# Loading the adaLN modulation weights in half-size column blocks, earlier, and one part of them later

## The chip, the cores and the metric

The kernel runs on one core of a Trainium2 chip. The metric is the device time of one execution in microseconds. TensorE is called PE here, its weight loads PEld, VectorE DVE, ScalarE ACT, GpSimd POOL and SyncE SP. Each engine takes its instructions in order from a queue of its own. SP issues nearly all DMAs.

## The reference: what is computed

Two layers over 256 latent and 256 context tokens of width 1024, in float32. Each layer has six modulation vectors (shift, scale and gate for the mixer, and again for the experts) per condition:

```python
cond_l = silu(c); cond_c = silu(c_ctx)
shift1, scale1, gate1, shift2, scale2, gate2 = split(cond_l @ mod_w[layer] + mod_b[layer], 6)
h = layer_norm(x) * (1 + scale1) + shift1
x = post_norm(ALPHA * x + gate1 * token_mixer(h), ...)
h = layer_norm(x) * (1 + scale2) + shift2
x = post_norm(ALPHA * x + gate2 * moe(h), ...)
```

`mod_w` is 2 x 1024 x 6144. The token mixer projects `h` with `w_in`, runs four branches (windowed attention, a bidirectional Mamba-2 scan, global attention, S5), gates and sums them (`merge`), and multiplies by `w_out`. The experts are 32, with two per token, chosen by a router.

## The kernel before

The work is written out layer by layer in `mixer` and `moe`. A scheduler of the kernel framework turns that text into one fixed order per engine when the kernel is built. It goes by data dependences, by buffers that come free, and by a priority, which is the place in the text; `tc.high_priority(offset=n)` moves what stands inside it n instructions ahead. The attention (scores, softmax, transposes, products) stands in such a block of 3000, because it is traced behind the projections but has a long chain.

The modulation of one layer is cut into three parts i = 0, 1, 2 of 2048 columns of `mod_w`, two vectors each. Part 0 gives shift1 and scale1, which the layer needs first; part 1 gives gate1 and shift2; part 2 gives scale2 and gate2. `mod_part(l, i, ...)` (through `mod_steps`) does a part in eight steps, one for 128 rows of the weight: a DMA of 128 x 2048 floats (1 MB, 8 KB per row) into the tile `modr` (L162), then four matmuls of 512 columns into four groups of 32 rows of the PSUM tile `pm` (L164). The two conditions stand in `cond`, padded to 32 columns. Behind the eighth step DVE adds the bias `mb`, four DMAs store the rows in the DRAM tensor `mods`, and for part 0 `mod_scalars` transposes them into `modT`, from which the layer's first normalisation takes its scalars.

Part (0, 0) is done at the start. The loop behind the attention traces parts (0, 1), (0, 2) and (1, 0) in layer 0, and (1, 1) and (1, 2) in layer 1. The pool `modr` has one buffer, so a load needs the matmuls of the load before it to be over. The PSUM pool `psM` of `pm` has one buffer too; the router's `pcv` and `pcs` use it behind the parts.

Then comes `merge`, a loop over the branches in the order 1, 3, 0, 2: `yr` loads a branch's rows (two buffers), `yh` and `yl` split them for a three-product float32 matmul (L507 to L509), `raw`, `hi` and `lo` do the same to `w_branch`, `gatel` loads the gates, and DVE adds the gated result to `msum`. Behind the second branch stands the router's preparation: `cv` loads shift2 and scale2 from `mods`, `pcv` transposes them, and `wc` and `csum` are built in buffers of `yr`. Behind the merge `pmod.close()` gives the space of `modr` free, `rawo`, `woh` and `wol` prepare `w_out`, and `pout` is the output projection.

Of the kernel before, what the change touches and what calls it, by code (L numbers as in the profile page):

```python
# [11 lines left out]
F32 = mybir.dt.float32  # L12
# [10 lines left out]
KT = 8  # L23
# [15 lines left out]
def part_bcast(ap, n):  # L39

    return bass.AP(tensor=ap.tensor, offset=ap.offset, ap=[[0, n]] + [list(d) for d in ap.ap])
# [11 lines left out]
def trunk(ctx: ExitStack, tc: tile.TileContext, A, out):  # L53
    nc = tc.nc
    V, S, G, T = nc.vector, nc.scalar, nc.gpsimd, nc.tensor
    dma = nc.sync.dma_start
# [8 lines left out]
    def pa(name="pa"):  # L65
        return psA.tile([128, 512], F32, tag="a", name=name)
# [7 lines left out]
    def pm_(name="pm"):  # L74
        return psM.tile([128, 512], F32, tag="m", name=name)

    def tt(o, a, b, op):
        V.tensor_tensor(o, a, b, op=op)  # L78
# [59 lines left out]
    cond = const.tile([128, KT, 32], F32, name="cond")  # L138
# [11 lines left out]
    def mod_part(l, i, wtile, width, mbt):  # L150

        return [ld for ld in mod_steps(l, i, wtile, width, mbt)][-1]

    def mod_steps(l, i, wtile, width, mbt):

        pm = pm_("pm")
        n = width // 512
        for kt in range(KT):
            for j0 in range(0, 4, n):
                w = wtile()  # L160
                c0 = i * 2048 + j0 * 512
                ld = dma(w, A["mod_w"][l, kt * 128:(kt + 1) * 128, c0:c0 + width])  # L162
                for j in range(n):
                    T.matmul(pm[32 * (j0 + j):32 * (j0 + j) + 32, :], cond[:, kt, :], w[:, j * 512:(j + 1) * 512],  # L164
                             start=(kt == 0), stop=(kt == KT - 1))
                yield ld
        mb = mbt()
        V.memset(mb, 0.0)
        for j in range(4):
            src = A["mod_b"][l, (4 * i + j) * 512:(4 * i + j + 1) * 512]  # L170
            dma(mb[32 * j:32 * j + 2], part_bcast(src, 2))
        row = mb
        tt(row, pm, mb, OP.add)
        for j in range(4):
            dma(mods[l, 4 * i + j], row[32 * j:32 * j + 2])
        if i == 0:
            mod_scalars(l, row)
# [3 lines left out]
    def mod_scalars(l, row):  # L181

        pt = pm_("pmt").rearrange("p (a b) -> p a b", a=4)
        for q in range(4):
            T.transpose(pt[:, q], row[:, q * 128:(q + 1) * 128], ident)
        V.tensor_copy(modT[l], pt.rearrange("p q (j r) -> p q j r", j=4)[:, :, :, 0:2])
        ts(modT[l][:, :, 2:4], modT[l][:, :, 2:4], 1.0, None, OP.add)
# [238 lines left out]
    def mixer(l, keep, prev):  # L426
# [6 lines left out]
        gates = pg_.enter_context(tc.tile_pool(name=f"gates{l}", bufs=1, reuse_waits="tile"))  # L433
# [6 lines left out]
        with ExitStack() as pl_:  # L440
# [33 lines left out]
            if prev:  # L474
                prev[1].close()
                modr = pmod.enter_context(tc.tile_pool(name=f"modr{l}", bufs=1, side="right", reuse_waits="tile"))
# [26 lines left out]
        def load_w(c0, n):  # L503
            return [split_w(A["w_in"][l, half * 512:(half + 1) * 512, c0:c0 + n], n) for half in range(2)]
# [86 lines left out]
        w = load_w(C_SB, 256)  # L591
        for i, p in enumerate(proj_fm(w, 0)):
            conv(4 + i, p, 0)
        w = load_w(C_SC, 272)
# [8 lines left out]
        for kt in range(KT):  # L603
            for i, b in enumerate((hhi, hlo)):
                T.matmul(pdf[:32], wdt[:, kt].rearrange("p i c -> p (i c)"), b[:, kt], start=(kt == 0 and i == 0),
                         stop=(kt == KT - 1 and i == 1))
# [35 lines left out]
        for ck in range(2):  # L642
            w = load_w(C_SZ + 256 * ck, 256)
# [7 lines left out]
        with tc.tile_pool(name=f"us{l}", bufs=2, reuse_waits="tile") as wk:  # L651
            for ck in range(2):
                w = load_w(C_SU + 256 * ck, 256)
# [233 lines left out]
        for br, c_q, c_k in ((0, C_AQ, C_AK), (1, C_GQ, C_GK)):  # L887
            for ck in (2, 0, 1):
                w = load_w(c_q + 256 * ck if ck < 2 else c_k, 256)
                for t in range(0 if ck == 2 else t0 // 128, 4):  # L890
                    p = pa("ptm")
# [39 lines left out]
        for n in order:  # L931
            if n == order[3]:
                s5_glu()
            for ck in range(4):
                w = load_w(C_GATE + 1024 * n + 256 * ck, 256)
# [10 lines left out]
        else:  # L946
            tla = ptl.enter_context(tc.tile_pool(name=f"ta{l}", bufs=1, side="right", reuse_waits="tile"))
            modr = pmod.enter_context(tc.tile_pool(name=f"modr{l}", bufs=1, side="right", reuse_waits="tile"))
# [157 lines left out]
                        att_tile(ab[1], pp, wk, late.pop(0))  # L1106
            att_apply(*pend)

        for ml, mi in ((0, 1), (0, 2), (1, 0)) if l == 0 else ((1, 1), (1, 2)):
            mod_part(ml, mi, lambda: modr.tile([128, 2048], F32, tag="modr", name="modr"), 2048,  # L1110
                     lambda: gates.tile([128, 512], F32, tag="gate", name="mb", bufs=4) if l == 0 else modr.tile([128, 512], F32, tag="mb", name="mb"))

        g1 = {qt0 // 2: mod_bc(tla, l, 2, qt0 // 2, "g1")}

# [1 line left out]
        for n in order:  # L1116
# [13 lines left out]
            for ck in range(4):  # L1130
# [5 lines left out]
                for i in range(2):  # L1136
                    g = gates.tile([128, 512 - t0], F32, tag="gate", name="gatel", bufs=4)
                    dma(g, g_d[l, n, 2 * ck + i, :, t0:])
                    p = pa("pm")
# [10 lines left out]
            if n == order[1]:  # L1150
# [26 lines left out]
                T.matmul(pcs, ones, flat, start=True, stop=True)  # L1177
                V.tensor_copy(flat, pcs)


        nt = 4 - qt0
        pmod.close()
# [2 lines left out]
        with ExitStack() as pt_:  # L1185
# [44 lines left out]
            for t in range(nt):  # L1230
                tk = slice(128 * t, 128 * t + 128)
                c = (t + qt0) // 2
# [5 lines left out]
                h = bc.tile([128, D], F32, tag="h2", name="h2")  # L1238
                rt["x1"].append(x)
                for nh in range(2):  # L1240
                    cs = slice(512 * nh, 512 * nh + 512)
                    p = pa("pout")
# [7 lines left out]
                for half in range(2):  # L1250
                    pt = pb("ph2").rearrange("p (a b) -> p a b", a=4)
                    for a in range(4):
                        kt = 4 * half + a
# [690 lines left out]
    for l in range(L):  # L1944
        keep = ExitStack()
        rt = mixer(l, keep, prev)
        prev = moe(rt, keep), keep
# [78 lines left out]
```

## Time and profile before

| | |
|---|---|
| median of 3 runs | 2580.48 us (2578.58 to 2581.49) |
| the profiled execution | 2574.12 us |
| its span, first to last instruction | 2572.2 us |
| PE busy | 2199.5 us, 86% |
| DVE busy | 1403.1 us, 55% |
| ACT busy | 692.3 us, 27% |
| mean granted clock of PE | 0.936 |
| DMA | 710.66 MB, mean 276 GB/s |

Busy times of an engine are the time that its instructions covered; those of PE have modelled ends, since matmuls are pipelined. A wait is the idle time of an engine ahead of an instruction, with what ended it. The granted clock is PE's, as a share of its upper level of 2.4 GHz; 0.5 is the lower one, 1.2 GHz. Times in the rows below are from the span's start. The layers' mixers run from 0 to about 960 us and from about 1540 to 2080 us, each with its experts behind it.

### The profile page before, as it was taken

The numbers are of one execution on the slowest core, as the hardware profiler recorded it, in microseconds if no ns is written. First come the engines' busy times: TensorE is split into PE (matmuls) and PEld (weight loads), VectorE is DVE, ScalarE is ACT, GpSimd is POOL, SyncE is SP. The second block draws the span as 40 slices with busy tenths as digits, with TensorE's granted clock in tenths as the row PEclk, the third lists the DMA queues.
The fourth block names the chain that finished last, engine by engine and source line by source line (L and its number), as shares of the span: only waits on it lengthen the run. The fifth ranks groups of instructions, "written<-read, shape, count | busy, mean of one in ns | idle before, by whom it ended". The sixth has DMA issues, their size and how long they took to land. (4 is left out here: it accounts for less than half of the span.)

```text
span 2572.2 us, 40839 instructions
## 1 busy us (share of the span) xinstructions
PE 2199.5 (86%) x15878; PEld 1514.0 (59%) x15878; DVE 1403.1 (55%) x2787; ACT 692.3 (27%) x1344; POOL 724.5 (28%) x686
## 2 busy tenths in 40 slices
PE   5898997799994988987888747997889879999996
PEld 3687875576651765544444427886777755555553
DVE  7947889956761782000000058466679665454544
ACT  2334422144551301111111113352456311111110
POOL 8989787753210031111111020201133110000000
PEclk8999998899996988999999978998999879999998
DMA  6643477675764768999999965459875689999996
GB/s 247 179 145 120 131 212 199 172 243 169 224 191 159 245 242 347 372 412 407 416 405 415 411 258 171 148 183 262 272 244 149 217 322 384 422 422 421 422 421 271
DMA packets 290516, 710.66 MB, mean 276 GB/s; under 512 B 40014, under 2 KB 199166, under 8 KB 232464
## 3 DMA queue, kind: packets, MB, share of 16 engines
q1 hardware_dynamic: 283600, 694.72, 74.8%
q0 software_dynamic: 5280, 8.05, 1.1%
q10 hardware_dynamic: 1440, 5.24, 0.5%
q8 instruction: 127, 2.08, 0.3%
q14 instruction: 69, 0.57, 0.1%
HBM read 645.82 MB, written 71.37 MB: 279 GB/s over the span
## 5 line engine op out<-in xcount | busy, mean ns | idle before, releaser
L1706 PE MATMUL pgu<-mraw,xgt 128*64 128x256 f32 x4224 | 494.4, 385 | 30.1 <-DMA mraw<-in_moe_w_up_dram 27.0
L1706 PEld LDWEIGHTS pgu<-mraw,xgt 128*64 128x64 f32 x4224 | 298.7, 138 | 220.2 <-DMA mraw<-in_moe_w_up_dram 57.5
L84 DVE SCALAR_TENSOR_TENSOR th<-th,pgu 128x256 f32<-128x256 f32 x132 | 55.5, 421 | 500.5 <-ACT th L1671 498.2
L507 PE MATMUL pfm<-hhi,hi 128*128 128x256 f32 (+1 forms) x832 | 282.9, 344 | 6.0 <-ACT hi L93 4.6
L1726 PE MATMUL pd<-mraw,at 128*64 128x512 f32 x1056 | 251.7, 604 | 39.9 <-DMA mraw<-in_moe_w_down_dram 38.0
L509 PE MATMUL pfm<-hhi,lo 128*128 128x256 f32 (+1 forms) x832 | 280.8, 342 | 4.9 <-DVE lo L78 4.8
L508 PE MATMUL pfm<-hlo,hi 128*128 128x256 f32 (+1 forms) x832 | 283.1, 342 | 2.1 <-DVE hlo L78 2.0
L78 DVE TENSOR_TENSOR lo<-raw,hi 128x1024 fp32r<-128x1024 f32 (+1 forms) x147 | 207.1, 1412 | 74.9 <-ACT hi L93 74.0
L128 POOL TENSOR_TENSOR bnrs<-bnrs,mhalf 128x1 f32<-128x1 f32 x26 | 29.1, 1125 | 688.3 <-DVE bnrs L88 688.3
L93 ACT ACTIVATE hi<-raw 128x1024 fp32r<-128x1024 f32 (+1 forms) x160 | 169.4, 1059 | 195.4 <-PE pfm L508 99.5
L1726 PEld LDWEIGHTS pd<-mraw,at 128*64 128x64 f32 x1056 | 72.2, 136 | 182.1 <-issue 112.7
L507 PEld LDWEIGHTS pfm<-hhi,hi 128*128 128x128 f32 x832 | 158.7, 193 | 33.9 <-ACT hi L93 5.2
L509 PEld LDWEIGHTS pfm<-hhi,lo 128*128 128x128 f32 x832 | 157.6, 191 | 27.2 <-DVE lo L78 6.3
L508 PEld LDWEIGHTS pfm<-hlo,hi 128*128 128x128 f32 x832 | 158.5, 191 | 20.4 <-DVE hlo L78 2.9
L78 DVE TENSOR_TENSOR acc<-acc,po 128x512 f32<-128x512 f32 x124 | 79.6, 683 | 99.7 <-PE po L1814 99.6
L1766 POOL DMA_INDIRECT yb_d<-ye,idx x30 | 29.9, 998 | 294.0 <-ACT ye L93 266.7
L507 PE MATMUL pm<-yh,hi 128*128 128x512 f32 (+1 forms) x256 | 88.5, 360 | 11.6 <-DVE gatel L84 6.4
L508 PE MATMUL pm<-yl,hi 128*128 128x512 f32 (+1 forms) x256 | 91.0, 357 | 5.0 <-DVE yl L78 4.9
L164 PE MATMUL pm<-modr,cond 128*32 128x512 f32 x320 | 61.2, 684 | 38.4 <-DMA modr<-in_mod_w_dram 38.3
L507 PE MATMUL ptm<-hi,hhi 128*128 128x256 f32 x320 | 92.5, 289 | 0.0
L509 PE MATMUL ptm<-hi,hlo 128*128 128x256 f32 x320 | 91.7, 287 | 0.0
L508 PE MATMUL ptm<-lo,hhi 128*128 128x256 f32 x320 | 91.7, 287 | 0.0
(506 smaller groups left out, 4354.9 us busy)
## 6 DMA issues: line engine op xcount, KB each, us to landing
mraw<-in_moe_w_gate_dram SPq DMA_DIRECT2D x132, 1024.0 KB
mraw<-in_moe_w_up_dram SPq DMA_DIRECT2D x132, 1024.0 KB
mraw<-in_moe_w_down_dram SPq DMA_DIRECT2D x132, 1024.0 KB
raw<-in_w_in_dram SPq DMA_DIRECT2D x116, 512.0 KB
modr<-in_mod_w_dram SPq DMA_DIRECT2D x40, 1024.0 KB
modw<-in_mod_w_dram SPq DMA_DIRECT2D x8, 1024.0 KB
gt_d<-gt SPq DMA_DIRECT2D x16, 512.0 KB
q_d<-Q SPq DMA_DIRECT2D x32, 256.0 KB
```

The source lines that it names most:

```text
L78: V.tensor_tensor(o, a, b, op=op)
L84: V.scalar_tensor_tensor(o, a, s, b, op0=op0, op1=op1)
L93: S.activation(o, a, AF.Copy, scale=scale)
L128: G.tensor_tensor(o, a, b, op=OP.pow)
L164: T.matmul(pm[32 * (j0 + j):32 * (j0 + j) + 32, :], cond[:, kt, :], w[:, j * 512:(j + 1) * 512], start=(kt == 0), stop=(kt == KT - 1))
L507: T.matmul(p, ahi, bhi, start=first, stop=False)
L508: T.matmul(p, ahi, blo, start=False, stop=False)
L509: T.matmul(p, alo, bhi, start=False, stop=last)
L1706: o = T.matmul(p[64 * cb:64 * cb + 64, 256 * i:256 * i + 256], xt[:, kt], raw[:, k, 256 * cb:256 * cb + 256], start=(kt == 0), stop=(kt == ...
L1726: o = T.matmul(p[64 * nh:64 * nh + 64], at[:, j, 64 * cb:64 * cb + 64], raws[cb][:, j, nh], start=(k == 0), stop=(k == 3))
L1766: sc_ = G.indirect_dma_start(out=yb_d.rearrange("r (n c) -> (r n) c", n=2), out_offset=bass.IndirectOffsetOnAxis(ap=i, axis=0), in_=y, in_ ...
```

## The change

Parts (l, 1) and (l, 2) are now traced in a block of priority 6000, ahead of the attention's 3000. Their weights come in sixteen loads each instead of eight: for each half h of the four groups of 512 columns and each 128 rows, a DMA of 128 x 4 x 256 floats (512 KB, in pieces of 1 KB). `modr` has two such buffers, together as large as the one before. A step has four matmuls of 256 columns. The first half's eight steps come first, then the second's. Part (1, 0) is no longer in the same loop. It is traced in layer 0 behind the whole merge loop, with the same priority block. The bias, the stores and `mod_scalars` are the same (`mod_end`). Part (0, 0) is as before.

```diff
+        mod_end(l, i, pm, mbt)
+
+    def mod_cols(l, i, wtile, mbt):
+
+        pm = pm_("pm")
+        for h in range(2):
+            for kt in range(KT):
+                w = wtile()
+                dma(w, A["mod_w"][l, kt * 128:(kt + 1) * 128, i * 2048:i * 2048 + 2048]
+                    .rearrange("p (j h c) -> p j h c", j=4, h=2)[:, :, h])
+                for j in range(4):
+                    T.matmul(pm[32 * j:32 * j + 32, 256 * h:256 * h + 256], cond[:, kt, :], w[:, j],
+                             start=(kt == 0), stop=(kt == KT - 1))
+        mod_end(l, i, pm, mbt)
+
+    def mod_end(l, i, pm, mbt):
         mb = mbt()
         V.memset(mb, 0.0)
...
-        for ml, mi in ((0, 1), (0, 2), (1, 0)) if l == 0 else ((1, 1), (1, 2)):
-            mod_part(ml, mi, lambda: modr.tile([128, 2048], F32, tag="modr", name="modr"), 2048,
-                     lambda: gates.tile([128, 512], F32, tag="gate", name="mb", bufs=4) if l == 0 else modr.tile([128, 512], F32, tag="mb", name="mb"))
+        def mods_of(*parts):
+
+            with tc.high_priority(offset=6000):
+                for ml, mi in parts:
+                    mod_cols(ml, mi, lambda: modr.tile([128, 4, 256], F32, tag="modr", name="modr", bufs=2),
+                             lambda: gates.tile([128, 512], F32, tag="gate", name="mb", bufs=4) if l == 0 else modr.tile([128, 512], F32, tag="mb", name="mb"))
+
+        mods_of((l, 1), (l, 2))
...
                 T.matmul(pcs, ones, flat, start=True, stop=True)
                 V.tensor_copy(flat, pcs)
 
+        if l == 0:
+            mods_of((1, 0))
 
         nt = 4 - qt0
         pmod.close()
```

The scheduler makes other orders of this. Lines below the new functions are 16 to 23 higher in the changed kernel: its L523 to L525 are L507 to L509 of the kernel before, and L178 is the matmul of `mod_cols`.

PE in layer 0, at the end of the attention, before (`ppt` and `po` are its transposes and products, `pm<-modr` the modulation, `pm<-yh` the third branch's merge):

```order
L1071 MATMUL ppt<-identr,P 128x128 x20
L1078 MATMUL po<-PT,vv 64x512 x8
L164 MATMUL pm<-modr,cond 32x512 x24
L185 MATMUL pmt<-identr,mb 128x128 x4
L1164 MATMUL pcv<-identr,cv 128x32
L1177 MATMUL pcs<-csum,ones 128x128
L507 MATMUL pm<-yh,hi 128x512 x2
```

The last six megabytes of modulation, the transposes of part (1, 0) and the router's two matmuls stood between the last attention product and the third merge.

PE in the changed kernel, where the router's second matmul now stands (`psc` are scores of the global attention):

```order
L1087 MATMUL ppt<-identr,P 128x128 x4
L1198 MATMUL pcs<-csum,ones 128x128
L1053 MATMUL psc<-kT,qT 128x512
L1057 MATMUL psc<-kT,qT 128x512
L1094 MATMUL po<-PT,vv 64x512 x4
L178 MATMUL pm<-modr,cond 32x256 x8
L523 MATMUL pm<-yh,hi 128x512 x2
L1053 MATMUL psc<-kT,qT 128x512
L1057 MATMUL psc<-kT,qT 128x512
```

The third merge begins among the scores, and part (1, 0) begins there too; `pcv` stands 20 rows further up. The end of the same stretch:

```order
L178 MATMUL pm<-modr,cond 32x256 x8
L1087 MATMUL ppt<-identr,P 128x128 x12
L178 MATMUL pm<-modr,cond 32x256 x4
L1094 MATMUL po<-PT,vv 64x512 x8
L178 MATMUL pm<-modr,cond 32x256 x4
L523 MATMUL pm<-yh,hi 128x512 x2
```

The last group of part (1, 0) follows the last attention product, with the fourth merge directly behind it.

SP at the start of layer 1, before (`gtl` to `Ml` are the S5 tables):

```order
L801 DMA gtl<-gt_d 128x2048
L803 DMA Wl<-w_d 128x1024
L805 DMA Rl<-r_d 128x512
L808 DMA Ql<-q_d 64x4x512 x2
L811 DMA Ml<-strip_d 16x8x128 x8
L162 DMA modr<-in_mod_w_dram 128x2048
L171 DMA mb<-in_mod_b_dram 2x512 x4
```

and in the changed kernel:

```order
L175 DMA modr<-in_mod_w_dram 128x4x256 x2
L817 DMA gtl<-gt_d 128x2048
L187 DMA mb<-in_mod_b_dram 2x512 x4
L819 DMA Wl<-w_d 128x1024
L821 DMA Rl<-r_d 128x512
L824 DMA Ql<-q_d 64x4x512 x2
L175 DMA modr<-in_mod_w_dram 128x4x256
L827 DMA Ml<-strip_d 16x8x128 x2
L175 DMA modr<-in_mod_w_dram 128x4x256
```

The modulation loads of layer 1 go ahead of the S5 tables; all 32 of them stand among the `w_in` loads of the first projections, where nine of the sixteen stood before.

## Rows read from the trace of the kernel before

**Rows 1.** The page's table of 40 equal slices, in tenths: PE busy, DMA share.

```profile
PE   5898997799994988987888747997889879999996
...
DMA  6643477675764768999999965459875689999996
```

**Rows 2.** Stretches: length, busy us of PE, PEld, DVE, ACT, POOL, clock, DMA share, GB/s.

```profile
740.00:780.00 40.00, 38.24 (x201) 17.91 (x198) 21.75 (x66) 28.66 (x78) 11.70 (x14) 1.00 0.57 182
780.00:840.00 60.00, 27.58 (x125) 11.24 (x125) 9.94 (x21) 4.87 (x8) 0.00 (x0) 0.63 0.44 151
```

**Rows 3.** Timeline of PE behind the attention: start, us, what, [idle before <-releaser].

```profile
786.37 4.41 PE L1078 MATMUL po<-PT,vv 128*64 128x512 f32 x16
790.71 1.07 PE L164 MATMUL pm<-modr,cond 128*32 128x512 f32 x8
796.68 1.94 PE L164 MATMUL pm<-modr,cond 128*32 128x512 f32 x8 [4.91 <-DMA modr<-in_mod_w_dram]
...
824.17 1.94 PE L164 MATMUL pm<-modr,cond 128*32 128x512 f32 x8 [5.04 <-DMA modr<-in_mod_w_dram]
826.92 1.11 PE L185 MATMUL pmt<-identr,mb 128*128 128x128 f32 x4 [0.81 <-DVE mb L78]
828.32 0.31 PE L1164 MATMUL pcv<-identr,cv 32*128 32x32 f32 x1 [0.28 <-DVE modT L186]
...
835.24 1.22 PE L507 MATMUL pm<-yh,hi 128*128 128x512 f32 x2 [1.91 <-ACT yh L93]
```

**Rows 4.** Waits from 790 to 840: who <- for what, us, times, longest.

```profile
ACT yh L93 <- DMA yr<-y_d: 50.3, 3, 47.5
...
PE pm L164 <- DMA modr<-in_mod_w_dram: 24.7, 5, 5.0
```

**Rows 5.** Timeline of SP in the same stretch.

```profile
783.10 36.41 SPq L162 DMA_DIRECT2D modr<-in_mod_w_dram  x6
...
831.89 0.32 SPq L1123 DMA_DIRECT2D yr<-y_d  x1
```

**Rows 6.** The page's costliest groups: the modulation matmuls, busy, mean ns, idle before.

```profile
L164 PE MATMUL pm<-modr,cond 128*32 128x512 f32 x320 | 61.2, 684 | 38.4 <-DMA modr<-in_mod_w_dram 38.3
```

**Rows 7.** Stretches of layer 1, columns as in the second group.

```profile
1560.00:1740.00 180.00, 180.00 (x1287) 154.65 (x1286) 107.87 (x208) 80.06 (x148) 17.33 (x5) 0.99 0.53 166
1740.00:1880.00 140.00, 113.41 (x1099) 97.31 (x1099) 92.02 (x195) 44.78 (x78) 14.70 (x7) 0.90 0.92 276
```

**Rows 8.** Waits from 1800 to 1880.

```profile
PE pm L164 <- DMA modr<-in_mod_w_dram: 8.6, 3, 5.4
```

**Rows 9.** Timeline of PE: merge of the third branch, then the first output projection.

```profile
843.40 0.40 PE L508 MATMUL pm<-yl,hi 128*128 128x512 f32 x1
...
847.80 0.39 PE L509 MATMUL pm<-yh,lo 128*128 128x512 f32 x1
...
887.01 0.47 PE L507 MATMUL pout<-woh,m 128*128 128x512 f32 x1 [0.59 <-DVE gatel L84]
```

**Rows 10.** DVE's groups by shape from 836 to 890: busy, mean ns, idle before.

```profile
L78 DVE TENSOR_TENSOR msum<-msum,gatel 128x512 f32<-128x512 f32 x16 | 10.9, 689 | 0.2
L84 DVE SCALAR_TENSOR_TENSOR gatel<-gatel,pm 128x512 f32<-128x512 f32 x16 | 10.8, 684 | 4.2 <-PE pm L509 4.2
L78 DVE TENSOR_TENSOR wol<-rawo,woh 128x1024 fp32r<-128x1024 f32 x8 | 9.8, 1224 | 2.6 <-ACT woh L93 2.6
...
L84 DVE SCALAR_TENSOR_TENSOR m<-msum,m 128x512 fp32r<-128x512 f32 x5 | 3.3, 686 | 0.7 <-ACT m L93 0.7
```

**Rows 11.** Timelines of SP and ACT: one 512 KB load and its reader.

```profile
862.21 0.38 SPq L1196 DMA_DIRECT2D rawo<-in_w_out_dram  x1
...
865.63 1.06 ACT L93 ACTIVATE woh<-rawo 128x1024 fp32r<-128x1024 f32 x1 [1.19 <-DMA rawo<-in_w_out_dram]
```

**Rows 12.** Stretches of layer 1, modulation alone: length, PE, PEld, clock, DMA share, GB/s.

```profile
1572.00:1757.00 185.00, 12.71 (x72) 1.81 (x72) 1.00 0.55 170
1757.00:1870.00 113.00, 8.33 (x56) 1.15 (x56) 0.91 0.91 281
```

## The prediction

> **What bounds the kernel now.** I read the page's table of 40 slices first. TensorE (PE) is 80% to 90% busy nearly everywhere, but slice 12 falls to 4 while the DMA share there is only 4 too [rows 1]. So neither PE nor the memory is the limit in that slice, and somebody waits for a latency. The table of stretches puts it between 780 and 840 us: PE is busy for 27.58 of 60 us at a mean granted clock of 0.63, VectorE (DVE) for 9.94, and the DMA share is 0.44 [rows 2]. PE's timeline says what happens. The last attention product ends at 790.71. Then come six groups of modulation matmuls, the last five 6.9 us apart, each preceded by about 4.9 us of idle time that a `modr` load ends. The first merge matmul of the third branch starts only at 835.24, behind the router's `pcv` transpose at 828.32 [rows 3]. The table of waits confirms it twice: PE waited 24.7 us for `modr`, and ScalarE 50.3 us for `yr`, the rows of the next branch [rows 4]. SyncE shows why `yr` was late: it stood 36.41 us at the last six `modr` loads, each needing the one buffer that the matmuls before had to free, and `yr` was queued behind [rows 5]. Over the whole program PE waits 38.3 us for `modr` [rows 6].
>
> In layer 1 the same weights come as sixteen more loads. PE is busy for all 180 us from 1560 to 1740 at a DMA share of 0.53; from 1740 to 1880 it is busy for 113.41 of 140 us at a DMA share of 0.92 [rows 7]. PE waits 8.6 us for `modr` there, in three places [rows 8].
>
> **Layer 0, the part that leaves the hole.** The change moves part (1, 0), eight of the 24 megabytes, behind the router's block, and gives (0, 1) and (0, 2) priority over the softmax work. The orders show `pcv` and `pcs` among the scores of the last attention tiles, and the third branch's merge among them too. I price the stretch from 790.71 to the first output projection at 887.01, which is 96.3 us [rows 3, 9]. What must still run on PE of it:
> - Six megabytes of modulation matmuls, 1.07 us each at the full clock as at 790.71 [rows 3]: 6.4 us. A half-width group moves half as many columns, so two halves are priced as one group of before; the trace has no such group, so this is an estimate, with 0.5 us more per megabyte as the upper end.
> - `pmt`, `pcv` and `pcs`: the first two took 1.11 and 0.31 us at the lower clock [rows 3]; about 1.5 for all three at the full one.
> - The third branch's 96 matmuls. From 843.40 to 847.80 lie 19 steps, 0.232 us each [rows 9]: 22.3 us. I take it as fully added to the attention, since PE is busy for 38.24 of 40 us from 740 to 780 [rows 2]. Those busy times have modelled ends, so some of the merge may fill real pauses: down to about 12 us as the lower end.
> - The fourth branch, which needs the last attention tile, and the preparation of W_out. On PE it is 22.3 us, but DVE must in the same time do eight pairs of `gatel` and `msum` (8 x 1.37), eight `wol` (8 x 1.22), one `lo` of the same shape (1.22) and eight `m` copies (8 x 0.69) [rows 10]: 11.0 + 9.8 + 1.2 + 5.5 = 27.5 us. DVE is what is late next, so this piece costs 28 us.
>
> Together 6.4 + 1.5 + 22.3 + 28 = 58.2 against 96.3: **38 us less**. The cover for the moved part (1, 0) is the attention and the third merge; without it, it would cost eight times 6.9 us again.
>
> **What is added in layer 0.** The part (1, 0) now ends just ahead of the fourth merge, and its bias loads and `mods` stores stand on SyncE ahead of the `sc`, `sh`, `g` and `z` loads; before, `z` went first. DVE has an add that waits for a bias of 4 KB issued a few instructions earlier. Both are near the first output tile. I take 2 us, between 0 and 5.
>
> **The loads themselves.** Forty loads of 1 MB become eighty of 512 KB, in rows of 1 KB. A 1 MB load, once its buffer is free, costs PE about 4.9 us of idle time [rows 3]. A 512 KB load with rows of 1 KB went from issue at 862.21 to its reader's start at 865.63 in 3.42 us, with the reader waiting for it [rows 11]. With two buffers a load is on the way while the other is used, so a megabyte needs some 4.5 us against 6.9. The Trainium skill, "DMA: Bandwidth & Descriptors" (Bandwidth), speaks against this change: batch transfers to 1 MiB or more. By the fit in its section on the anatomy of one DMA (made for transfers that GpSimd issues: 2.0 us fixed, the rest by size) 1 MiB takes 4.4 us and 512 KiB 3.2, so that forty megabytes in halves, one after the other, would load 80 us longer: an estimate from that page. The trace agrees on the sizes (4.9 and 3.42 us).
>
> Elsewhere in layer 0 PE waited 38.3 - 24.7 - 8.6 = 5.0 us for `modr` [rows 4, 6, 8]. Now 32 half-loads stand between the glu, the last gates and the first merges, about as close together as two loads allow. I take 5 us of new waits for the 5 that go; the ends are 0 and 20.
>
> **Layer 1.** Of the sixteen groups (eight records each) nine ran before 1757 and seven after, 12.71 and 8.33 us of PE [rows 12]. All sixteen megabytes now stand in the first projections, so PE gets up to 8 us more in a stretch where it has no pause [rows 7]. The later stretch loses that work, the 8.6 us of waits, and 7 MB from DMA queues that are 0.92 busy. I take 14 us less there and 8 more in front: **6 us less**, between 14 less and 10 more (waits at the new groups).
>
> **Sum.** -38 + 2 + 0 - 6 = -42. Against the profiled execution's 2574.12 us that gives 2532. The median of the runs is 2580.48, 6.4 above it, so I put the median at about **2538 us**. The work behind the merge (output projection, routing, experts) I cost at nothing: it starts earlier as a whole, and its weight loads begin when buffers come free there.
>
> **Rivals.**
> *The loads stall the in-order queues (slower).* Every group is a wait on PE with projections, gates or scores queued behind, and every load is a wait on SyncE with `raw`, `gatel` and `yr` behind. Where DMA is busy, three 1 MB loads cost 8.6 us [rows 8], 2.9 each. There are now 40 pairs of halves in three dense stretches. Break-even is 42 / 40, or 1.05 us per pair. With 2.9 us at half of them, 58 us are added and the result is 2538 + 58 = 2596. For it: in front of layer 1 PE has no pause [rows 7], and sixteen megabytes now arrive where nine did. Against it: a DMA share of 0.53 there [rows 7], and two buffers. This is what the Trainium skill's rule on transfer size would lead to.
> *The attention stretches.* If the softmax chain (ScalarE is busy for 28.66 of 40 us [rows 2]) is slowed by the third merge's `hi`, `yh`, `lo` and `yl`, the tail moves out, by about the 18 us of DVE work that the merge brings: 2538 + 18 = 2556, still faster.
> *It doesn't happen.* The order is fixed when the kernel is built. If the real loads are later than it expects, part (1, 0) ends behind the attention after all. Six megabytes at 4.9 us of idle time [rows 3] bring back 29 us, layer 1 at its upper end another 10, and the result is 2577, the same as before.
>
> **How the numbers follow.** The forecast has 0.78, the stretched attention 0.12, nothing gained 0.04, the stalls 0.06. A measurement of this kernel can tell 0.2%, about 5 us, from no change. Faster by more than that: 0.78 + 0.12 = 0.90; within: 0.04; slower: 0.06. For the range, the forecast's own ends are -10 (merge woven into pauses), -5 (no new waits) and -8 (layer 1), which rarely all meet: 2515. Upward the other faster case ends near 2556, and 10 us of waits or of layer 1 put it at 2563. What lies beyond is less than 2 in 10.
>
> **What would show it.** Right: no `modr` wait on PE behind the last attention product; `pcv` before it; merge matmuls within a few microseconds of it; slice 12 at 8 or 9; the first output projection near 849; in layer 1 no `modr` load behind the first `qkv_d` stores. Wrong: PE rows of the half-width groups each with 1 us or more of idle time that `modr` ends; `hi` of layer 1's first projections waiting for `raw` longer than before; or a fourth merge that takes 40 us because DVE is behind.

## The result, and the profile of the changed kernel

The changed kernel took 2547.67 us (median of 4 runs, 2545.33 to 2550.55) against 2580.88 for the kernel before, beside which it ran: a ratio of 0.9873, with a 95% interval of 0.9859 to 0.9886. It is 33 us faster; 42 were forecast. The time lies in the stated range, 10 us above the predicted value, and the parts of the sum did not come out alike: layer 0 gained more than forecast, and layer 1 lost where a gain was forecast.

The page's table of 40 slices, PE busy and DMA share, of the changed kernel (a slice is 63.6 us):

```profile
PE   5898997799999979878888829998789879999996
...
DMA  6644476678767679999999958649664699999996
```

Slice 12 has 9 and 7 where [rows 1] had 4 and 4: the hole is gone. Stretches of 60 us, with the columns of [rows 2] (length, PE, PEld, DVE, ACT and POOL busy, clock, DMA share, GB/s):

```profile
780.00:840.00 60.00, 53.58 (x280) 34.63 (x279) 40.24 (x57) 21.93 (x33) 3.34 (x2) 1.00 0.64 205
```

PE is busy for 53.58 us instead of 27.58, at the full clock instead of 0.63. PE's timeline at the end of the attention:

```profile
806.57 0.64 PE L178 MATMUL pm<-modr,cond 128*32 128x256 f32 x8 [1.14 <-DMA modr<-in_mod_w_dram]
807.14 3.65 PE L1094 MATMUL po<-PT,vv 128*64 128x512 f32 x16
810.72 0.64 PE L178 MATMUL pm<-modr,cond 128*32 128x256 f32 x8
811.29 0.73 PE L523 MATMUL pm<-yh,hi 128*128 128x512 f32 x2
```

The last attention product starts at 807.14 and is over at 810.72 (790.71 in [rows 3]). One half-size group of part (1, 0) follows, and the fourth merge starts at 811.29. The first output projection:

```profile
837.88 0.47 PE L523 MATMUL pout<-woh,m 128*128 128x512 f32 x1 [1.14 <-DVE gatel L84]
```

It came at 887.01 before [rows 9]. Waits from 560 to 860 us (who <- for what, us, times, longest), and the page's group of the modulation matmuls:

```profile
ACT yh L93 <- DMA yr<-y_d: 8.7, 6, 3.9
...
PE pm L178 <- DMA modr<-in_mod_w_dram: 4.1, 5, 1.5
```

```profile
L178 PE MATMUL pm<-modr,cond 128*32 128x256 f32 x640 | 50.7, 393 | 7.8 <-DMA modr<-in_mod_w_dram 7.8
```

PE's waits for `modr` fell from 38.3 us [rows 6] to 7.8, over 80 loads. ScalarE's one wait of 47.5 us for `yr` [rows 4] is gone with the loads that stood ahead of it [rows 5].

Layer 1 goes the other way. These are lengths between the same instructions on PE, from the start of each, in us, for both kernels and four that the experiments bring ("end" is the last output product of layer 1's experts):

| stretch | before | changed | changed, run again | layer 1 as before | priority only | changed, 1 MB loads |
|---|---|---|---|---|---|---|
| start to first output projection | 887.0 | 837.9 | 835.5 | 838.2 | 841.9 | 838.1 |
| to the first expert matmul | 89.0 | 92.3 | 92.1 | 92.4 | 88.4 | 92.8 |
| to layer 1's first projection | 584.3 | 589.1 | 584.8 | 584.4 | 585.0 | 585.8 |
| to the first S5 product (`pE`) | 197.3 | 216.9 | 217.4 | 197.9 | 204.0 | 199.8 |
| to the last attention product | 250.6 | 238.5 | 241.3 | 251.8 | 241.2 | 243.4 |
| to the end | 549.0 | 555.5 | 550.7 | 557.0 | 555.6 | 551.7 |

Two stretches vary between executions of one text: the third (589.1 and 584.8 for the changed kernel) and the last (549.0 to 557.0, over code that none of these edits touch). Differences of that size there are not read as effects. The fifth moved by 2.8 us between the two executions of the changed kernel. The fourth stretch is where the change costs: 19.6 us more. The trace splits it. The projections, then the modulation in that stretch, before (lengths, PE, PEld, DVE and ACT busy, clock, DMA share, GB/s; PE and PEld alone for the modulation):

```profile
1560.30:1757.60 197.30, 100.33 (x668) 90.37 (x668) 1.67 (x4) 10.78 (x23) 1.00 0.58 175
...
1560.30:1757.60 197.30, 12.71 (x72) 1.81 (x72) 1.00 0.58 175
```

and the same two of the changed kernel:

```profile
1519.30:1736.20 216.90, 111.18 (x703) 95.98 (x703) 1.61 (x4) 11.53 (x25) 0.99 0.68 200
...
1519.30:1736.20 216.90, 20.89 (x256) 5.08 (x256) 0.99 0.68 200
```

The modulation has 8.2 us more there, as forecast. But 703 projection matmuls now stand ahead of the first S5 product where 668 stood; the projections have 10.9 us more; and PE, which never paused in that stretch, idles for 3.7 us. (The three add up to more than 19.6 us, since busy times of modulation and projections overlap: all of PE's work together is 15.9 us more.) Most of the idle time is one wait. The group that waited took 0.64 us, and the next one 1.08, at the lower clock; the granted clock from 1539 to 1559 is 0.91:

```profile
1547.96 0.64 PE L178 MATMUL pm<-modr,cond 128*32 128x256 f32 x8 [2.91 <-DMA modr<-in_mod_w_dram]
...
1549.78 1.08 PE L178 MATMUL pm<-modr,cond 128*32 128x256 f32 x8
```

### The profile page after: what moved, and what is told of

Same layout as the page of the kernel before. It is cut to its first block, busy times and chain, and to the rows that moved or that the text cites. A ratio compares the mean times of both kernels' runs of the same rounds, so it can differ in the third digit from the quotient of the medians.

```text
span 2545.2 us, 41555 instructions
## 1 busy us (share of the span) xinstructions
PE 2204.2 (87%) x16198; PEld 1523.7 (60%) x16198; DVE 1396.3 (55%) x2787; ACT 693.5 (27%) x1344; POOL 719.0 (28%) x686
## 5 line engine op out<-in xcount | busy, mean ns | idle before, releaser
L1749 PE MATMUL pd<-mraw,at 128*64 128x512 f32 x1056 | 253.2, 608 | 43.6 <-DMA mraw<-in_moe_w_down_dram 41.7
L525 PE MATMUL pfm<-hhi,lo 128*128 128x256 f32 (+1 forms) x832 | 283.5, 344 | 7.8 <-DVE lo L78 7.2
L523 PE MATMUL pfm<-hhi,hi 128*128 128x256 f32 (+1 forms) x832 | 284.9, 346 | 4.9 <-ACT hi L93 4.3
L525 PEld LDWEIGHTS pfm<-hhi,lo 128*128 128x128 f32 x832 | 158.9, 192 | 31.5 <-DVE lo L78 8.8
L523 PEld LDWEIGHTS pfm<-hhi,hi 128*128 128x128 f32 x832 | 159.4, 193 | 29.3 <-issue 7.0
L523 PE MATMUL pm<-yh,hi 128*128 128x512 f32 (+1 forms) x256 | 88.1, 360 | 11.3 <-DVE gatel L84 7.0
L523 PE MATMUL ptm<-hi,hhi 128*128 128x256 f32 x320 | 92.7, 291 | 0.0
L84 DVE SCALAR_TENSOR_TENSOR yg<-pd,wcol,g 64x512 f32<-64x512 f32 x64 | 48.0, 749 | 79.7 <-PE pd L1749 79.2
L525 PE MATMUL ptm<-hi,hlo 128*128 128x256 f32 x320 | 91.6, 287 | 0.0
```

What stands on the lines that cost most here:

```text
L84: V.scalar_tensor_tensor(o, a, s, b, op0=op0, op1=op1)
L523: T.matmul(p, ahi, bhi, start=first, stop=False)
L525: T.matmul(p, alo, bhi, start=False, stop=last)
L1749: o = T.matmul(p[64 * nh:64 * nh + 64], at[:, j, 64 * cb:64 * cb + 64], raws[cb][:, j, nh], start=(k == 0), stop=(k == 3))
```

## The experiments

Each kernel was timed against the kernel before on the same chip; ratios are given with their 95% interval, since chips differ by a few us.

### Which layer gains

The first run gives layer 1 its old text, the second gives it to layer 0.

```diff
-        mods_of((l, 1), (l, 2))
+        if l == 0:
+            mods_of((0, 1), (0, 2))
+        else:
+            for mi in (1, 2):
+                mod_part(1, mi, lambda: modr.tile([128, 2048], F32, tag="modr", name="modr"), 2048,
+                         lambda: modr.tile([128, 512], F32, tag="mb", name="mb"))
```

> Layer 0 as changed, layer 1 as before (parts (1,1) and (1,2) in 1 MB loads, one buffer, no priority). Theory A, the new order costs time in layer 1: the lead over the kernel before was 41 us when layer 1 began and 27 at the end, so 14 us come back: about 2534, with 2530 to 2540 allowed. In its trace the first S5 product starts 197 us after layer 1's first projection, as before, not 217. Rival B, layer 1 is longer for another cause (clock, or what layer 0 leaves behind): within 4 us of 2548.

Measured: 2538.96 us, 0.9842 (0.9829 to 0.9855). The front of layer 1 is 197.9 us long, as theory A said. The gain on the changed kernel, some 8 us by the two ratios, is less than the 14 named: 4.7 of those lay in the third stretch of the table, which varies by itself.

> The other half: layer 0 as before (three parts of 1 MB loads in one place), layer 1 as changed. Theory A: the kernel before plus 14 us, 2595 (2589 to 2600). Rival B: 2581 within 4 us. Rival C, my forecast for layer 1 (6 us less): 2575.

Measured: 2586.11 us, 1.0041 (1.0023 to 1.0058), so layer 1's part alone is slower than the kernel before by 6 us; its front takes 213.5 us. C falls, and so does A with its 14 us; the median lies between the ranges of A and B, 1 us above B's, and by the interval, which lies above 1, the part does cost time. The projections in that front (columns as in the rows above):

```profile
1559.20:1772.70 213.50, 108.63 (x703) 94.11 (x703) 1.67 (x4) 11.56 (x25) 1.00 0.70 203
```

Both runs agree: layer 0 is worth about -41 us, layer 1 about +6 to +9.

### Which of the three edits closes the hole in layer 0

The third run leaves part (1, 0) with the others.

```diff
-        mods_of((l, 1), (l, 2))
+        mods_of(*([(l, 1), (l, 2)] + ([(1, 0)] if l == 0 else [])))
...
-        if l == 0:
-            mods_of((1, 0))
```

> The changed kernel with part (1,0) left in the block of the other parts, with their priority and half-size loads. Theory A: what closes the hole in layer 0 is that the loads run ahead of the softmax work, not where (1,0) is traced; its eight megabytes still end before the last attention product, so 2548 within 5 us. Rival D: the move is what frees the third merge; with 24 MB ahead of it the merge and the router's transposes start later than the attention ends and 10 to 25 us come back, 2558 to 2573.

Measured: 2543.06 us, 0.986 (0.9846 to 0.9875). D falls: the first expert matmul starts at 930.4, against 930.2 in the changed kernel. With the priority and half-size loads, the place of (1, 0) is worth nothing there.

The fourth takes the kernel before and changes the loads alone (`mod_cols` for `mod_part` in the old loop, two buffers, no priority).

> The kernel before with half-size loads in two buffers alone: no priority, no moved part. Theory A': the two buffers alone let the modulation keep pace in the gaps of the attention; in the built order none of it stands behind the last attention product, so 25 to 40 us go, 2541 to 2556, the better because layer 1 keeps its old placement. Rival E: without priority the real loads come late and PE still waits for them near the end of the attention (20 us or more of waits for modr): 2560 to 2580.

Measured: 2556.19 us, 0.9909 (0.9894 to 0.9923), at the upper edge of theory A'. PE waits only 7.0 us for `modr` in layer 0, and yet the first expert matmul comes at 952.4, 22 us later than in the changed kernel. PE's timeline at the end of the attention:

```profile
801.74 3.83 PE L1094 MATMUL po<-PT,vv 128*64 128x512 f32 x16
805.50 0.66 PE L201 MATMUL pmt<-identr,mb 128*128 128x128 f32 x4
806.44 0.24 PE L1180 MATMUL pcv<-identr,cv 32*128 32x32 f32 x1 [0.29 <-DVE modT L202]
810.60 0.79 PE L1193 MATMUL pcs<-csum,ones 128*128 128x128 f32 x2 [3.91 <-DVE csum L1191]
813.22 1.22 PE L523 MATMUL pm<-yh,hi 128*128 128x512 f32 x2 [1.83 <-ACT yh L93]
```

The loads keep pace, but the parts end together with the attention, and that ends at 805.5, 15 us later than before. `pcv` and `pcs` come behind it, and the third merge starts 7.7 us behind the attention's end, at the lower clock. From the attention's end to the output projection 60 us remain of 96. The attention's later end takes part of that back, and 24 us are left at the first expert matmul, where the change gains 46. The next run shows where the rest lies.

The fifth has the priority and nothing else, with 1 MB loads and one buffer.

```diff
-        for ml, mi in ((0, 1), (0, 2), (1, 0)) if l == 0 else ((1, 1), (1, 2)):
-            mod_part(ml, mi, ...
+        with tc.high_priority(offset=6000):
+            for ml, mi in ((0, 1), (0, 2), (1, 0)) if l == 0 else ((1, 1), (1, 2)):
+                mod_part(ml, mi, ...
```

> The kernel before with priority 6000 for its parts alone: 1 MB loads, one buffer, (1,0) in the same place as the others. 24 serial loads at 6.9 us each need 165 us and start when the pool opens near 570 us, so they end near 735 to 750, ahead of the last attention product. Theory A: an early start is enough in layer 0; its lead when the experts begin is 40 us as in the changed kernel, layer 1 loses 6 to 10 as in the second experiment: 2545 to 2552. Rival H: with one buffer each group stalls PE for up to 4.9 us wherever PE gets ahead of the loads, with projections and scores queued behind: 20 us or more of modr waits in layer 0 and as many in front of layer 1, 2560 to 2580.

Measured: 2529.7 us, 0.9805 (0.9791 to 0.982), faster than the changed kernel by 18 us and better than theory A said: the lead at the first expert matmul is 46 us instead of 40, and layer 1 up to its last attention product is 2.7 us shorter than before (table), where 6 to 10 more were expected. Its modr waits in layer 0 are 5.9 us, in layer 1 none. H falls. All 24 serial loads were done before the last attention product:

```profile
784.21 3.99 PE L1078 MATMUL po<-PT,vv 128*64 128x512 f32 x16 [0.34 <-DVE PT L1072]
788.13 0.49 PE L1178 MATMUL pcs<-csum,ones 128*128 128x128 f32 x2
789.33 0.73 PE L507 MATMUL pm<-yh,hi 128*128 128x512 f32 x2 [0.71 <-ACT yh L93]
```

Here two merges follow the attention, the third and the fourth, up to the output projection at 841.9. The matmuls into `pm` in that stretch, then in the same stretch of the changed kernel, where eight of the 104 are modulation and one merge remains (lengths, PE, PEld and DVE busy, clock, DMA share, GB/s):

```profile
788.20:841.90 53.70, 47.98 (x192) 35.08 (x192) 10.09 (x15) 1.00 0.68 210
```

```profile
810.70:837.90 27.20, 23.95 (x104) 17.81 (x104) 4.85 (x8) 1.00 0.47 155
```

So the third merge under the attention gains nothing at the first expert matmul: with it the attention ends 23 us later, the first output projection comes 4 us earlier, and the experts begin at the same time (930.2 and 930.3). What closes the hole is that the modulation with its waits is done before the attention ends; and with the priority the attention ends no later for it (788.1, against 790.7 before). Against the halves alone, the attention ends 17 us earlier and the third merge follows 6.5 us closer; from there to the output projection both take 52 to 53 us. Why the attention ends so much later with the halves alone is not settled.

The sixth moves part (1, 0) behind the merge and changes nothing else.

> The kernel before with part (1,0) traced behind the merge and nothing else: 1 MB loads, one buffer, no priority. In the built order six of its eight groups still stand between the last attention product and the output projection, now among the merge matmuls, and one behind. Theory A: the third merge starts under the attention, but six loads at 6.9 us still come behind it, and PE has only the fourth merge (22 us) to cover them: 15 to 25 us less than before, 2555 to 2565. Rival I: the move alone does the whole work of layer 0, 2538 to 2545 (layer 1 is as before here). Rival J: the loads of (1,0) hold the merge's rows back on SP's queue: 2575 or more.

Measured: 2545.46 us, 0.9871 (0.9855 to 0.9887), between theory A and I, 0.5 us above I's range. The first expert matmul comes at 945.0, 31 us before the old time. Six groups follow the last attention product, and PE needs to wait once, since the merge matmuls cover the rest:

```profile
800.38 1.07 PE L164 MATMUL pm<-modr,cond 128*32 128x512 f32 x8
...
828.22 1.06 PE L164 MATMUL pm<-modr,cond 128*32 128x512 f32 x8 [2.29 <-DMA modr<-in_mod_w_dram]
...
847.79 1.06 PE L164 MATMUL pm<-modr,cond 128*32 128x512 f32 x8
```

So each of the three edits alone takes away much of the hole (at the first expert matmul: halves 24 us, move 31, priority 46), they don't add up, and with the priority the other two add nothing there.

### Layer 1: the gap between the layers, and the changed kernel again

PE waits 38.33 us for the first normalisation of layer 1. The seventh run puts part (1, 1) there (half-size loads, a pool of its own opened at the start of layer 1's mixer).

```diff
+            if l == 1:
+                with tc.high_priority(offset=0):
+                    for mi in (1,):
+                        mod_cols(1, mi, lambda: modg.tile([128, 4, 256], F32, tag="modr", name="modr", bufs=2), ...
             with tc.high_priority(offset=400 * l):
                 h_in(0)
```

> Layer 0 as changed; in layer 1 part (1,1) is traced at the mixer's start, in half-size loads into a pool of its own, so that 8 MB stand in the 38 us in which PE waits for the first normalisation of layer 1; part (1,2) stays behind the attention in 1 MB loads, one buffer, no priority. Theory A (what costs in layer 1 is PE time in its busy front, and waits for loads in the S5 stretch): against the first experiment, 2539, PE's 8 us for (1,1) move into idle time, and the granted clock no longer drops to 0.5 ahead of the first projections: 4 to 12 us less, 2527 to 2535. Rival K: the loads delay what the gap waits for (the rows of the experts' output and the first w_in loads on the same queue): 2539 to 2550.

Measured: 2541.98 us, 0.9858 (0.9841 to 0.9876), in K's range. The interval overlaps the first experiment's (0.9829 to 0.9855), so a loss against it is not shown, but the gain of 4 us or more is excluded. From the S5 stage to the last attention product it needs 243.5 us against the first experiment's 251.8, but the first projection starts 49.3 us behind the last expert product instead of 43.6. SP holds the loads back behind the stores of the experts' output (`x_d`), and the longest wait for `modr` falls there:

```profile
1482.71 9.76 SPq L175 DMA_DIRECT2D modr<-in_mod_w_dram  x4
1500.49 1.53 SPq L1974 DMA_DIRECT2D x_d<-fa  x2
1502.13 6.23 SPq L175 DMA_DIRECT2D modr<-in_mod_w_dram  x3
```

Three of the half-size groups, the last three rows below, stand among the transposes of the normalisation, each with a wait:

```profile
1506.85 1.08 PE L178 MATMUL pm<-modr,cond 128*32 128x256 f32 x8 [8.51 <-DMA modr<-in_mod_w_dram]
...
1514.68 1.08 PE L178 MATMUL pm<-modr,cond 128*32 128x256 f32 x8 [0.73 <-DMA modr<-in_mod_w_dram]
...
1518.78 0.64 PE L178 MATMUL pm<-modr,cond 128*32 128x256 f32 x8 [0.90 <-DMA modr<-in_mod_w_dram]
...
1521.42 1.08 PE L178 MATMUL pm<-modr,cond 128*32 128x256 f32 x8 [1.41 <-DMA modr<-in_mod_w_dram]
```

The clock did not rise in the gap either: from 1481 to 1515 the granted clock is 0.50.

> The changed kernel once more, on the same chip as the three above, to compare with the third experiment (part (1,0) early, 2543) and to see whether the 5 us that its layer-0 experts took longer than in the first and third experiment come back. If they belong to that one execution: 2541 to 2546 and 540 to 541 us for the experts of layer 0. If they belong to the kernel: 2546 to 2550 and 545 us.

Measured: 2549.07 us (2538.61 to 2552.9), 0.9891 (0.9876 to 0.9905). The profiled execution, the fastest, has 541.3 us for the experts, so the 545.8 belong to the other execution. But the median stayed, so that does not explain the distance to the third experiment, and 2543 against 2549 stays unclear; neither of the two cases named holds.

### What the halving costs

The ninth run is the changed kernel with 1 MB loads in one buffer: `mod_part` in `mods_of`, priority and late part (1, 0) kept.

> The changed kernel with its loads back at 1 MB in one buffer: priority and the late part (1,0) stay. Theory L, after the fifth experiment: the halving earns nothing in layer 0 and costs 10 to 18 us in layer 1, so this stands near the priority alone (2530), 2526 to 2536, and its modr waits stay under 10 us. Rival A, the halves carry part of the gain: 2545 or more. Where (1,0) stands should not matter by more than 5 us between this and the fifth experiment.

Measured: 2531.98 us, 0.9833 (0.9814 to 0.9852). Theory L holds: without the halving the changed kernel is faster by 10 us by the ratio of its first measurement (0.9873) and by 15 by that of the second (0.9891). Layer 0 is as long as with halves (first expert matmul at 930.9), and the front of layer 1 takes 199.8 us, with no pause; its projections and modulation there:

```profile
1516.70:1716.50 199.80, 99.14 (x663) 89.16 (x663) 1.67 (x4) 10.72 (x23) 1.00 0.69 208
...
1516.70:1716.50 199.80, 17.05 (x128) 2.52 (x128) 1.00 0.69 208
```

All sixteen megabytes are in front here too, but 663 projection matmuls instead of 703. The tenth and eleventh run ask whether the pieces or the two buffers do it; both start from the fifth. In the tenth the load's source and the matmuls' operands follow the tile's shape.

```diff
-            ... modr.tile([128, 2048], F32, tag="modr", name="modr"), 2048,
+            ... modr.tile([128, 8, 260], F32, tag="modr", name="modr")[:, :, :256], 2048,
```

> The fifth experiment (priority, 1 MB loads, one buffer) with each load cut into pieces of 1 KB by a buffer whose rows have a gap behind every 256 floats; the built order is the same instruction for instruction. Theory M, the small pieces are what the half-size loads cost (they hold the DMA engines longer, and the projections' weights come later): 2538 to 2546, and modr waits above the fifth experiment's 6 us. Rival N, it is the order that the scheduler makes of 32 loads in two buffers (33 more projection matmuls ahead of the S5 stage, a 2.9 us wait early in layer 1): within 3 us of 2530.

Measured: 2540.9 us (2533.39 to 2542.77), 0.9854 (0.9834 to 0.9873), 11 us above the fifth, in the same order of instructions. M holds, N as sole cause falls. PE's waits for `modr` are 8.9 us against 5.9. The profiled execution (2535.7 us with what lies around its span of 2533.9) shows 3 us of the loss in layer 0 and 3 in front of layer 1; where the rest of the median's 11 us lies, no trace shows. The DMA engines are held longer for the same bytes. The attention of layer 0, 1 MB loads in 8 KB rows, then in 1 KB pieces:

```profile
565.00:790.00 225.00, 213.62 (x1143) 138.70 (x1141) 149.39 (x339) 118.82 (x279) 50.55 (x48) 0.98 0.71 231
```

```profile
568.00:793.00 225.00, 211.16 (x1137) 136.93 (x1137) 148.77 (x338) 118.84 (x279) 50.53 (x48) 0.98 0.75 230
```

A share of 0.75 against 0.71 for 230 and 231 GB/s. The loads in question are 24 of the 52 MB that this stretch moves.

The eleventh run has two buffers of 1 MB in layer 1.

```diff
-            ... modr.tile([128, 2048], F32, tag="modr", name="modr"), 2048,
+            ... modr.tile([128, 2048], F32, tag="modr", name="modr", bufs=1 + l), 2048,
```

> The fifth experiment with two buffers of 1 MB in layer 1 (layer 0 has no room for a second). Loads then run ahead without being smaller: half of the sixteen groups stand before the 300th projection matmul, against the 475th with one buffer. Theory N (the loads running ahead delay the projections): the front of layer 1, from the first projection to the first S5 product, grows from 204 to 210 us or more, and the time to 2535 to 2545. Theory M (pieces): 2530 within 3 us, or a few us less.

Measured: 2534.33 us (2532.95 to 2543.81), 0.9841 (0.982 to 0.9861). The median lies between the two ranges, 1 us from either. The front takes 206.7 us, 2.7 more than in the fifth and short of the 210 named. The count of projections is the telling row:

```profile
1514.30:1721.00 206.70, 108.05 (x703) 95.36 (x703) 1.67 (x4) 11.55 (x25) 0.99 0.68 208
```

703, as in the changed kernel; with one buffer it is 672 in the fifth and tenth. So beside the priority it is the second buffer that brings the projection matmuls ahead of the S5 stage (in the fourth run, with two buffers and no priority, the count is 672 too), and the pieces cost on top. A third part is the width: the same sixteen megabytes kept PE busy for 20.9 us in groups of 256 columns and 17.05 us in groups of 512. Of the 12.9 us that the front is longer in the changed kernel than in the fifth, the second buffer shows 2.7 and the pieces 3.3, each alone; how the rest is shared is not settled.

The twelfth run gives the priority to layer 0 alone.

> The fifth experiment with the priority in layer 0 alone; layer 1's two parts stand behind the attention as before. My forecast said that taking them ahead gains 6 us in layer 1 (14 less in the S5 stretch, 8 more in front). If that is right for loads of 1 MB: 2533 to 2538 here, against 2530. Rival O, layer 1 gains nothing by priority: 2530 within 2 us.

Measured: 2535.23 us (2527.54 to 2537.27), 0.983 (0.9811 to 0.985) against the fifth's 0.9805 (0.9791 to 0.982). The median is where my forecast for layer 1 put it, but the intervals overlap, and in the traces layer 1 up to its last attention product is not longer without the priority (442.2 against 445.2 us). Whether 1 MB loads gain by priority in layer 1 stays open; it is within 6 us.

## Why the prediction was right, and where a step failed

**The hole in layer 0: right, and larger.** The forecast was 38 us less at the first output projection; it is 49.1. The pieces stand as written. Behind the last attention product one branch's merge and W_out remain, and that takes 27.2 us (810.72 to 837.88) where 28 were set down for DVE's work. The attention ends 20 us later than before, not the 30.2 of the sum (6.4 + 1.5 + 22.3). That was the term that was too large, and the lower end that the text named for the third merge, 10 us less, fits it. But pauses are only part of it: from 560 us to the end of the attention PE's idle time fell from 10.1 to 7.0 us, and the granted clock rose from 0.99 to 1.00; the rest is not settled. Toward the first expert matmul 3.3 us were added; 2 were forecast. The cover for part (1, 0) that the prediction asked for was there, but it is not needed: in the third and fifth runs (1, 0) stands with the other parts, and the experts begin as early.

**The loads: right.** The rival that they stall the in-order queues needed 1.05 us per pair of halves; there are 7.8 us over 40 pairs, 0.2 each. The Trainium skill, "DMA: Bandwidth & Descriptors" (Bandwidth), asks for batches of 1 MiB or more. The 80 us that the page's fit would have added for serial loads don't show: PE's waits for `modr` are 7.8 us in all. But its direction holds: back at 1 MB the kernel is 10 to 15 us faster, though part of that is the second buffer's order and the narrower groups, and no run has loads of 512 KB in longer pieces. The same page's table of specifications gives 512 bytes as the least transfer for full rate; the tenth experiment does not bear that out for its case, since pieces of 1 KB held the engines for 0.75 of the time where rows of 8 KB took 0.71.

**Layer 1: the step that failed.** "I take 14 us less there and 8 more in front." The 14 measured 12.1 (250.6 to 238.5; 9.3 when run again), and the 8 of modulation measured 8.2. But the front grew by 19.6. The forecast counted only the moved instructions, and took the rest of the order for unchanged. The built order has 35 more projection matmuls ahead of the S5 stage. They went from a stretch in which PE idles anyway (between the first S5 product and the first gate product 112.6 us less 87.9 busy before, 103.4 less 75.7 after) into one where PE has no pause, so by the rate before (0.150 us each) they would cost 5.3 us. That is an estimate, and rather an upper one: in the eleventh run 31 more of them than in the fifth came with 2.7 us more. The other 5.6 of the 10.9 are a slower pace (0.158 us each). The lower clock behind the wait goes with part of that: in the second run, whose front has the same counts at a granted clock of 1.00, the 703 projections have 108.6 us instead of 111.2; the rest is not settled. 3.7 us of waits came in beside. Layer 1 costs 6 to 9 us by the first two experiments, where 6 less were forecast. The row that would have told it, the number of `pfm` matmuls ahead of the first `pE`, was there in the two orders.

**The credit.** The range held, and partly by luck: layer 0 gained 11 us more than forecast and layer 1 came out about 13 worse, and the two nearly cancel. (The range's upper end does not follow from its terms either: 2556 and 10 make 2566, not 2563; nothing hangs on it.) The prediction also treated the change as one. The experiments show that the priority alone gives the whole gain and more: the fifth kernel, with that alone, takes 2529.7 us, the lowest median of all. The halving, which gave the change its name, adds 10 to 15 us, and the moved part (1, 0) shows no gain beside the priority (0.9833 in the ninth run against 0.9805 in the fifth, with intervals that overlap).

## What to carry to other kernels

When a load waits for its buffer in a stretch where nothing else is ready, ask first whether the whole group can be started earlier; a second buffer only shortens a wait that need not be there. Work that is moved out of a stretch with idle time into one without is no longer free, and a scheduler moves more than the diff names: count the instructions ahead of the next stage in both orders. And undo the parts of a change one at a time: three edits that each close most of the same hole look alike together.

## What was not expected of the hardware

A modulation group of four column groups takes 1.00 us with 512 columns and 0.57 with 256 (start to next start, at the full clock), so halving the width costs 0.14 us per megabyte. With 24 of a stretch's 52 MB in pieces of 1 KB instead of rows of 8 KB, the DMA engines were held 6% longer in that stretch (0.75 against 0.71). By its packets, a row of 8 KB held an engine for 376 ns and a piece of 1 KB for 53 ns, which is 13% more for the same bytes. And seven runs of the changed kernel spread from 2538.6 to 2552.9 us, where five of the fifth kernel lie between 2527.5 and 2532.9; other kernels here spread by 3 to 12 us, and no run shows why.
